# Moving the loads of the modulation weights and of the second branch's tiles from SyncE's queue to GpSimd's, in the merge of a hybrid diffusion layer

## The chip, the cores and the metric

The kernel runs on one core of one Trainium2 chip. The metric is the device time of one execution in microseconds (us); lower is better. The core has a matrix engine (TensorE, PE in the rows), VectorE (DVE), ScalarE (ACT), GpSimd (POOL) and SyncE (SP), each of which takes its own instructions in order, and 16 DMA engines that all queues share. A transfer is issued by an instruction in the queue of some engine; here nearly all of them stand in SyncE's.

## The reference, cut to what matters

One layer of a diffusion backbone: 1024 latent tokens and 256 context tokens of 1024 channels go through a mixer with two branches (a recurrent one, "A", and a state-space one, "B"), whose outputs are projected, gated and merged, and then through a gated MLP. All is float32. The parts around the change:

```python
mx = jnp.split((sc @ ada_w[l] + ada_b[l])[:, None, :], 6, axis=-1)       # six modulation vectors
...
g = (y * jax.nn.silu(z.astype(jnp.float32))).reshape(bsz, seqlen, SSD_GROUPS, SSD_INNER // SSD_GROUPS)
g = g * lax.rsqrt(jnp.mean(g * g, axis=-1, keepdims=True) + EPS)
return (g.reshape(bsz, seqlen, SSD_INNER) * norm_w.astype(jnp.float32)).astype(z.dtype)
...
def merge(ya, lg, yb, xs, z, gt):
    ra = ((ya[0] + ya[1]).astype(lg.dtype) * jax.nn.gelu(lg)) @ lru_proj
    rb = ssd_output(yb[0] + yb[1], xs, z, ssd_d, ssd_norm_w) @ ssd_proj
    ga, gb = jnp.split(jax.nn.sigmoid(gt), 2, axis=-1)
    return (ga * ra + gb * rb) @ w_out
...
x = x + mx[2] * ox
hx2 = modulate(rmsnorm(x, norm_ffn_w[l]), mx[3], mx[4])
x = x + mx[5] * conv_ffn(...)
```

The first two modulation vectors (`mx[0]`, `mx[1]`) are made at the start of the kernel; the other four (4096 values) are made inside the merge, and are first wanted by the residual add behind the output projection.

## The kernel before, in words

Channels lie on the 128 partitions and tokens along the free dimension. Precision is kept by splitting each float32 operand into a high part, which TensorE takes at full rate, and the remainder: a product is three matmuls, high by high, high by low, low by high (`gdense`, line 125). Splitting a tile is one copy on ScalarE (`act`, line 163) and one subtraction on VectorE (`tt`, line 160). So each weight tile of 128 output channels costs one load (`raw`, line 82), one ScalarE copy (`whi`), one VectorE subtraction (`wlo`), and 48 matmuls for 1024 tokens: 8 blocks of 128 input channels, 3 products, 2 halves of the tokens.

The merge (`merge`) has 24 such tiles, then the output projection `wout` follows:

- 8 tiles of `lru_proj`. Branch A's result, stored earlier to DRAM, is loaded tile by tile (`M<-ad`, line 1025) and split into the tiles `A` (even numbers high, odd numbers low); all eight are wanted by the first weight tile. Behind each tile the sigmoid of a gate (`sg`, `ga`, line 1034) multiplies the product into `M` on VectorE.
- 16 tiles of `ssd_proj`, in two halves of 8 of its 16 input blocks each. Ahead of each half, branch B's result is loaded from DRAM in pieces of 128x512 (`gk<-gd`, line 1050, 16 a half), multiplied by its norm's weight and the group's reciprocal root (`rsb<-rsd`, line 1045, one broadcast load for four pieces) in one VectorE instruction (line 157), and split: the first half into the tiles `H`, the second into `A` again. `gk` has two buffers, `rsb` one.

Beside this the remaining modulation is computed (`ada_rest`): `crow`, the conditioning vector on all partitions (line 338), through SiLU, then 32 times a load of a weight row block of 512 KB (`adar<-in_ada`, line 342) and one VectorE multiply-and-sum against `crow` (line 343), called a reduction below. `adar` has one buffer, so a load can't be issued before the reduction ahead of it is over. `ada_rest_end` adds the bias; `wout`'s first residual add waits for it.

Nobody writes the order by hand here. The program is recorded, and a scheduler sets the order of the instructions on each engine from its own estimate of when each can run; weight loads and splits have priority (`prio`). What each engine then runs is fixed: an instruction whose input is late holds all that stand behind it on its engine.

Of the kernel before, what the change touches and what calls it, by code (L numbers as in the profile page):

```python
# [15 lines left out]
P = 128  # L16
# [29 lines left out]
class Builder:  # L46
# [287 lines left out]
    def ada_rest(self, p1):  # L334

        nc, A = self.nc, self.A
        crow = self.t(p1, 1024, "crow")
        nc.sync.dma_start(crow, A["crows"][0].partition_broadcast(P))
        self.act(crow, crow, AF.Silu)
        for i in range(32):  # L340
            w = self.t(p1, 1024, "adar")
            nc.sync.dma_start(w, A["ada2"][i])
            nc.vector.tensor_tensor_reduce(w, w, crow, 1.0, 0.0, op0=ALU.mult, op1=ALU.add,
                                           accum_out=self.mods[:, 16 + i : 17 + i])
            yield
# [670 lines left out]
    def merge(self, pA, pM):  # L1016

        nc, tc, A = self.nc, self.tc, self.A
        F = self.FULL
        with tc.tile_pool(name="mg1", bufs=1) as p1, tc.tile_pool(name="mg2", bufs=2) as p2:  # L1020
            ah = [self.t(pA, T, f"A{2 * k}", F32R) for k in range(8)]
            al = [self.t(pA, T, f"A{2 * k + 1}", F32R) for k in range(8)]
            for k in range(8):
                ak = self.t(pM, T, f"M{k}")
                nc.sync.dma_start(ak, self.a_d[k])
                self.split(ak, ah[k], al[k])
            mm = [self.t(pM, T, f"M{k}") for k in range(8)]
            for m in range(8):
                w = self.wload(A["lrup"][m])
                ps = self.halves()  # L1030
                self.dense(ps, w, ah, al, F)
                for i, (s, e) in enumerate(F):
                    ga = self.gate_room(p1)
                    nc.sync.dma_start(ga, self.gate_d[m, :, s:e])
                    self.act(ga, ga, AF.Sigmoid)
                    self.tt(mm[m][:, s:e], ga, ps[i])
            rest = self.ada_rest(p1)
            for half in range(2):
                pool, nm = (self.pH, "H") if half == 0 else (pA, "A")
                yh = [self.t(pool, T, f"{nm}{2 * i}", F32R) for i in range(8)]  # L1040
                yl = [self.t(pool, T, f"{nm}{2 * i + 1}", F32R) for i in range(8)]
                for g in range(2):
                    for hf, (s, e) in enumerate(F):
                        rsb = self.t(p1, H, "rsb")
                        nc.sync.dma_start(rsb, self.rs_d[2 * half + g, 4 * hf : 4 * hf + 4].rearrange("c p -> (c p)")
                                          .partition_broadcast(P))
                        for i in range(4 * g, 4 * g + 4):
                            k = half * 8 + i
                            gk = self.t(p2, H, "gk")
                            nc.sync.dma_start(gk, self.g_d[k, :, s:e])  # L1050
                            self.stt(gk, gk, self.v("ssd_norm_w", k), rsb, op0=ALU.mult, op1=ALU.mult)
                            self.split(gk, yh[i][:, s:e], yl[i][:, s:e])
                for m in range(8):
                    w = self.wload(A["ssdp"][m, half])
                    ps = self.halves()
                    self.dense(ps, w, yh, yl, F)
                    for i, (s, e) in enumerate(F):
                        gb = self.gate_room(p1)
                        nc.sync.dma_start(gb, self.gate_d[8 + m, :, s:e])
                        self.act(gb, gb, AF.Sigmoid)  # L1060
                        self.tt(gb, gb, ps[i])
                        self.tt(mm[m][:, s:e], mm[m][:, s:e], gb, op=ALU.add)
                        next(rest, None)
            self.ada_rest_end()
            mh, ml = [], []
            for k in range(8):
                h = self.t(self.pH, T, f"H{2 * k}", F32R)
                l = self.t(self.pH, T, f"H{2 * k + 1}", F32R)
                self.act(h, mm[k], AF.Copy)
                self.tt(l, mm[k], h.bitcast(F32), op=ALU.subtract)  # L1070
                mh.append(h)
                ml.append(l)
        return mh, ml
# [502 lines left out]
```

## Time and profile before

| | |
|---|---|
| median of 3 runs | 2314.39 us (2313.72 to 2317.71) |
| the profiled execution's own time | 2316.08 us |
| its span in the profile | 2314.3 us |
| TensorE busy | 2238.8 us, 97% of the span |
| VectorE, ScalarE, GpSimd busy | 1640.5, 1150.1 and 330.0 us |
| moved by DMA | 274.88 MB, mean 119 GB/s |

A page of the profile gives busy time by engine, then the span in 40 slices, then the chain of work that ended last, then groups of equal instructions with their mean time and the idle time of their engine ahead of them. "SPq" is SyncE's queue of transfer issues. A row of a timeline gives its start in us from the start of the span, its length, engine, line and operation, and in brackets how long the engine had been idle and what ended that.

### The profile page before, as it was taken

How to read it: one execution, taken by the hardware profiler on the slowest of the kernel's cores; microseconds unless marked ns; L12 is line 12 of the kernel's file. 1: busy time of each engine (PE TensorE's matmuls, PEld its weight loads, DVE VectorE, ACT ScalarE, POOL GpSimd, SP SyncE). 2: the span in 40 equal slices, each digit the busy share in tenths (PEclk: the TensorE clock that was granted, in tenths of full speed). 3: DMA queues.
4: the chain of work that ended last, by engine and by line, in shares of the span. 5: the costliest groups of instructions: out<-in, count | busy, mean ns of one | idle time of the engine just before them, and what ended most of it. 6: DMA issues, size and time to landing. Idle time of an engine off the chain costs nothing.

```text
span 2314.3 us, 29745 instructions
## 1 busy us (share of the span) xinstructions
PE 2238.8 (97%) x11290; PEld 1852.4 (80%) x11290; DVE 1640.5 (71%) x2617; ACT 1150.1 (50%) x1781; POOL 330.0 (14%) x254
## 2 busy tenths in 40 slices
PE   6999999999999999999999999999889999999998
PEld 3778878778888888888888878888668888878888
DVE  4887877789978858767875675547877777774335
ACT  4577667667666647646635332334434444442121
POOL 0000000000000000000000000000757777740000
PEclk7999999999999999999999999999999999999999
DMA  6322322145335333524427775542022222244212
GB/s 250 96 69 73 95 83 65 62 126 159 122 107 172 114 121 106 159 85 130 155 90 267 234 231 191 171 139 73 28 73 82 83 82 82 80 161 129 77 55 73
DMA packets 87795, 274.88 MB, mean 119 GB/s; under 512 B 10434, under 2 KB 16610, under 8 KB 82404
## 3 DMA queue, kind: packets, MB, share of 16 engines
q1 hardware_dynamic: 87648, 272.97, 36.9%
q8 instruction: 89, 1.46, 0.3%
q14 instruction: 54, 0.44, 0.1%
q10 hardware_dynamic: 4, 0.01, 0.0%
HBM read 233.86 MB, written 39.08 MB: 118 GB/s over the span
## 4 chain that ended last, share of the span: by engine, by line
PE 76%; DVE 13%; DMA 5%; ACT 3%; issue 2%; POOL 1%; SPq 0%; POOLq 0%; DVEq 0%; ACTq 0%
PE d L125 30%; PE s L125 18%; PE d L1220 11%; PE s L1220 5%; PE s L986 2%; DMA adar<-in_ada 2%; PE s L651 2%; ACT L L163 1%; DVE wlo L160 1%; PE s L978 1%; DVE L L160 1%; DMA gk<-gd 1%; PE s L927 1%; PE s L926 1%; DVE facc L157 1%
## 5 line engine op out<-in xcount | busy, mean ns | idle before, releaser
L125 PE MATMUL d<-H,whi 128*128 128x512 f32 x2496 | 700.8, 398 | 1.8 <-DVE H L160 1.0
L125 PEld LDWEIGHTS d<-H,whi 128*128 128x128 f32 x2496 | 457.0, 188 | 97.1 <-issue 6.0
L125 PE MATMUL d<-H,wlo 128*128 128x512 f32 x1248 | 392.8, 393 | 1.8 <-DVE wlo L160 1.8
L163 ACT ACTIVATE whi<-raw 128x1024 fp32r<-128x1024 f32 (+2 forms) x194 | 185.7, 959 | 270.7 <-PE s L125 115.4
L125 PEld LDWEIGHTS d<-H,wlo 128*128 128x128 f32 x1248 | 232.9, 188 | 51.6 <-DVE wlo L160 3.5
L157 DVE SCALAR_TENSOR_TENSOR facc<-d,vec,facc 128x945 f32<-128x945 f32 (+2 forms) x176 | 214.6, 1221 | 72.9 <-ACT facc L163 68.6
L160 DVE TENSOR_TENSOR wlo<-raw,whi 128x1024 fp32r<-128x1024 f32 (+1 forms) x154 | 187.5, 1220 | 81.2 <-ACT whi L163 74.4
L125 PE MATMUL s<-H,whi 128*128 128x512 f32 x672 | 202.6, 390 | 1.9 <-ACT whi L163 1.9
L163 ACT ACT_TABLE_LOAD x102 | 130.9, 1283 | 85.9 <-DVE cacc L157 28.7
L1133 POOL TENSOR_TENSOR ssq<-H,A 128x512 f32<-128x512 f32 x4 | 6.0, 1493 | 1162.8 <-ACT H L163 1158.6
L125 PEld LDWEIGHTS s<-H,whi 128*128 128x128 f32 x672 | 125.8, 188 | 29.2 <-ACT whi L163 2.8
L125 PE MATMUL s<-A,whi 128*128 128x512 f32 x480 | 138.2, 390 | 1.0 <-POOL A L1133 1.0
L157 DVE SCALAR_TENSOR_TENSOR M<-s,mods,M 128x512 f32<-128x512 f32 (+1 forms) x72 | 49.5, 690 | 120.4 <-PE s L125 120.3
L125 PE MATMUL s<-H,wlo 128*128 128x512 f32 x336 | 126.0, 391 | 2.1 <-DVE wlo L160 2.0
L125 PEld LDWEIGHTS s<-A,whi 128*128 128x128 f32 x480 | 90.1, 188 | 20.1 <-POOL A L1133 1.4
L157 DVE SCALAR_TENSOR_TENSOR E<-E,cst 128x128 f32<-128x128 f32 x256 | 81.3, 344 | 20.5 <-ACT E L163 20.5
L163 ACT ACTIVATE m<-GU,dtt 128x128 f32<-128x128 f32 x256 | 78.7, 389 | 34.5 <-PE s L978 29.3
L157 DVE SCALAR_TENSOR_TENSOR m<-GL,dtt,m 128x128 f32<-128x128 f32 x256 | 77.7, 346 | 20.3 <-ACT m L163 20.1
L1220 PE MATMUL d<-A,whi 128*128 128x512 f32 x372 | 91.3, 395 | 0.0
L1220 PE MATMUL d<-A,wlo 128*128 128x512 f32 x348 | 85.9, 397 | 5.2 <-ACT ssq L163 5.2
L163 ACT ACTIVATE E<-E,cst 128x128 f32<-128x128 f32 x256 | 80.4, 389 | 17.5 <-DMA E<-csd 17.4
L125 PE MATMUL s<-A,wlo 128*128 128x512 f32 x240 | 83.1, 390 | 0.8 <-DVE wlo L160 0.8
(337 smaller groups left out, 4288.2 us busy)
## 6 DMA issues: line engine op xcount, KB each, us to landing
raw<-in_w SPq DMA_DIRECT2D x92, 512.0 KB, 3.6
E<-csd SPq DMA_DIRECT2D x32, 1024.0 KB, 7.1
A<-in_wup SPq DMA_DIRECT2D x40, 512.0 KB, 4.1
R<-csd SPq DMA_DIRECT2D x64, 256.0 KB, 4.7
adar<-in_ada SPq DMA_DIRECT2D x32, 512.0 KB, 4.0
hd<-facc SPq DMA_DIRECT2D x22, 512.0 KB, 5.1
gated<-sg SPq DMA_DIRECT2D x32, 256.0 KB, 3.8
gd<-y SPq DMA_DIRECT2D x32, 256.0 KB, 2.4
```

Of the source, the lines that this page charges most:

```text
L125: nc.tensor.matmul(o, a[:, k, :], b[k][:, xo + s : xo + e], start=(k == 0 and i == 0), stop=(k == kn - 1 and i == 2))
L157: self.pin(self.nc.vector.scalar_tensor_tensor(out, in0, s, in1, op0=op0, op1=op1))
L160: return self.pin(self.nc.vector.tensor_tensor(out, a, b, op=op))
L163: return self.pin(self.nc.scalar.activation(out, in_, f, **kw))
L651: nc.tensor.matmul(pg, a[:, q, :], b[:, s:e], start=(i == 0), stop=(i == 2))
L926: nc.tensor.matmul(ps[:, s - s2, 0, :], btok[:, s, :], xw[:, 0, s, :], start=True, stop=True)
L927: nc.tensor.matmul(ps[:, s - s2, 1, :], btok[:, 7 - s, :], xw[:, 1, 7 - s, :], start=True, stop=True)
L978: nc.tensor.matmul(psy[q, c, :], self.xt[:, c0 + c, q], m[:, h, c, :], start=True, stop=True)
L986: nc.tensor.matmul(pso[:, c, :], S[:, cc if d == 0 else 7 - cc, d, :], CT[:, cc * P : (cc + 1) * P], start=True, stop=True)
L1133: self.pin(self.nc.gpsimd.tensor_tensor(out, a, b, op=op))
L1220: q = self.pin(self.nc.tensor.matmul(ps, a[:, k, :], b, start=(k == 0 and i == 0 and p in ("11", "12", "s3")), stop=(k == 3 and i == 2), s ...
```

## The change

Four lines call another engine's queue: the loads of `crow`, `adar`, `rsb` and `gk` are issued by GpSimd instead of SyncE. 73 transfers move (1, 32, 8 and 32 of them). Tiles, buffers and arithmetic stay.

```diff
@@ ada_rest
         crow = self.t(p1, 1024, "crow")
-        nc.sync.dma_start(crow, A["crows"][0].partition_broadcast(P))
+        nc.gpsimd.dma_start(crow, A["crows"][0].partition_broadcast(P))
         self.act(crow, crow, AF.Silu)
         for i in range(32):
             w = self.t(p1, 1024, "adar")
-            nc.sync.dma_start(w, A["ada2"][i])
+            nc.gpsimd.dma_start(w, A["ada2"][i])
             nc.vector.tensor_tensor_reduce(w, w, crow, 1.0, 0.0, op0=ALU.mult, op1=ALU.add,
                                            accum_out=self.mods[:, 16 + i : 17 + i])
@@ merge
                         rsb = self.t(p1, H, "rsb")
-                        nc.sync.dma_start(rsb, self.rs_d[2 * half + g, 4 * hf : 4 * hf + 4].rearrange("c p -> (c p)")
+                        nc.gpsimd.dma_start(rsb, self.rs_d[2 * half + g, 4 * hf : 4 * hf + 4].rearrange("c p -> (c p)")
                                           .partition_broadcast(P))
                         for i in range(4 * g, 4 * g + 4):
                             k = half * 8 + i
                             gk = self.t(p2, H, "gk")
-                            nc.sync.dma_start(gk, self.g_d[k, :, s:e])
+                            nc.gpsimd.dma_start(gk, self.g_d[k, :, s:e])
```

Because the scheduler sees other queues, it also sets other orders. TensorE's is the same, row for row. Three places where the others differ follow.

**SyncE's and GpSimd's queues, where the moved loads begin.** Before, SyncE, from the first moved load on (`raw` is a weight tile, `gated` the stored gates):

```order
L1045 DMA rsb_10992<-rsd_3572 128x512
L82 DMA raw_10658<-in_lrup 128x1024
L1050 DMA gk_10994<-gd_3571 128x512
L1050 DMA gk_10999<-gd_3571 128x512
L829 DMA gated_93<-sg_10393 128x512
L338 DMA crow_11140<-in_crows 128x1024
L342 DMA adar_11143<-in_ada 128x1024
```

With the change, GpSimd, whose last instruction ahead of them fills a constant early in the state-space stage:

```order
L241 MEMSET btok_3726 64x4
L1045 DMA rsb_10992<-rsd_3572 128x512
L1050 DMA gk_10994<-gd_3571 128x512
L1050 DMA gk_10999<-gd_3571 128x512
L338 DMA crow_11140<-in_crows 128x1024
L342 DMA adar_11143<-in_ada 128x1024
L1050 DMA gk_11004<-gd_3571 128x512
L1050 DMA gk_11009<-gd_3571 128x512
L342 DMA adar_11151<-in_ada 128x1024
L1045 DMA rsb_11014<-rsd_3572 128x512
```

The moved loads now stand behind one another only; before, weight tiles and gates stood between them.

**VectorE, at the start of the merge** (`grsr` is the last norm of the state-space stage, `A` the splits of branch A that the first tile wants). Before:

```order
L160 TENSOR_TENSOR grsr_10243<-grsr_10243,grsa_10242 128x8
L160 TENSOR_TENSOR A_1384_10420<-M_1392_10428,A_1376_10412 128x1024
L160 TENSOR_TENSOR wlo_1410_10471<-raw_10468,whi_1409_10470 128x1024
L160 TENSOR_TENSOR A_1385_10421<-M_1393_10432,A_1377_10413 128x1024
L160 TENSOR_TENSOR A_1386_10422<-M_1394_10436,A_1378_10414 128x1024
L160 TENSOR_TENSOR A_1387_10423<-M_1395_10440,A_1379_10415 128x1024
L160 TENSOR_TENSOR A_1388_10424<-M_1396_10444,A_1380_10416 128x1024
L160 TENSOR_TENSOR A_1389_10425<-M_1397_10448,A_1381_10417 128x1024
L160 TENSOR_TENSOR wlo_1416_10534<-raw_10531,whi_1415_10533 128x1024
L160 TENSOR_TENSOR A_1390_10426<-M_1398_10452,A_1382_10418 128x1024
L160 TENSOR_TENSOR A_1391_10427<-M_1399_10456,A_1383_10419 128x1024
L157 SCALAR_TENSOR_TENSOR gk_10994<-gk_10994,vec_72,rsb_10992 128x512
```

With the change, from the row behind the same `grsr`:

```order
L157 SCALAR_TENSOR_TENSOR gk_10994<-gk_10994,vec_72,rsb_10992 128x512
L157 SCALAR_TENSOR_TENSOR gk_10999<-gk_10999,vec_72,rsb_10992 128x512
L160 TENSOR_TENSOR A_1384_10420<-M_1392_10428,A_1376_10412 128x1024
L160 TENSOR_TENSOR wlo_1410_10471<-raw_10468,whi_1409_10470 128x1024
L160 TENSOR_TENSOR A_1385_10421<-M_1393_10432,A_1377_10413 128x1024
L160 TENSOR_TENSOR A_1386_10422<-M_1394_10436,A_1378_10414 128x1024
L160 TENSOR_TENSOR A_1387_10423<-M_1395_10440,A_1379_10415 128x1024
L160 TENSOR_TENSOR H_1468_10984<-gk_10994,H_1460_10976 128x512
L160 TENSOR_TENSOR H_1469_10985<-gk_10999,H_1461_10977 128x512
L343 ISA adar_11143,mods_78<-adar_11143,crow_11140 128x1024
L343 ISA mods_78 128x1
L160 TENSOR_TENSOR A_1388_10424<-M_1396_10444,A_1380_10416 128x1024
```

Then come two more `gk` products, `A_1389`, `wlo_1416`, `A_1390`, `A_1391` and the second reduction. Work of branch B and a reduction now stand ahead of branch A's last four splits.

**VectorE, at the split of the fourth weight tile** (`wlo_1429`, from `raw_10658`). Before, two reductions stand ahead of it, of `adar_11143` and `adar_11151`:

```order
L160 TENSOR_TENSOR H_1471_10987<-gk_11009,H_1463_10979 128x512
L343 ISA adar_11151,mods_78<-adar_11151,crow_11140 128x1024
L343 ISA mods_78 128x1
L160 TENSOR_TENSOR M_1401_10461<-sg_10587,s_10537 128x512
L160 TENSOR_TENSOR M_1401_10461<-ga_10591,s_10538 128x512
L160 TENSOR_TENSOR wlo_1429_10661<-raw_10658,whi_1428_10660 128x1024
```

With the change five do, of `adar_11143`, `adar_11151`, `adar_11215`, `adar_11223` and `adar_11286`:

```order
L160 TENSOR_TENSOR H_1469_10985<-gk_11021,H_1461_10977 128x512
L343 ISA adar_11286,mods_78<-adar_11286,crow_11140 128x1024
L343 ISA mods_78 128x1
L157 SCALAR_TENSOR_TENSOR gk_11026<-gk_11026,vec_72,rsb_11014 128x512
L160 TENSOR_TENSOR M_1401_10461<-sg_10587,s_10537 128x512
L160 TENSOR_TENSOR wlo_1429_10661<-raw_10658,whi_1428_10660 128x1024
```

The count goes on by two for each tile in both. The last reduction, the 32nd, stands ahead of the split of the 19th tile before, and of the 18th with the change.

## Rows read from the trace of the kernel before

**Rows 1.** The page: busy us by engine (share of the span), instructions; granted clock in tenths.

```profile
PE 2238.8 (97%) x11290; PEld 1852.4 (80%) x11290; DVE 1640.5 (71%) x2617; ACT 1150.1 (50%) x1781; POOL 330.0 (14%) x254
...
PEclk7999999999999999999999999999999999999999
```

**Rows 2.** Windows over the merge, by stage: busy us (count) of each engine, clock, DMA share, GB/s.

```profile
1237.20:1325.50 88.30, 87.51 (x385) 71.92 (x384) 58.15 (x83) 35.58 (x49) 0.00 (x0) 1.00 0.74 242
1325.50:1422.10 96.60, 90.30 (x386) 71.43 (x385) 65.46 (x100) 26.22 (x38) 0.00 (x0) 1.00 0.68 222
1422.10:1509.00 86.90, 86.90 (x386) 71.93 (x385) 44.79 (x60) 26.93 (x34) 0.00 (x0) 1.00 0.55 175
```

**Rows 3.** Timeline of TensorE: first matmuls of merge and output projection, the longest stall.

```profile
1237.21 1.07 PE L125 MATMUL d<-A,whi 128*128 128x512 f32 x4
...
1338.28 1.20 PE L125 MATMUL s<-H,whi 128*128 128x512 f32 x4 [1.71 <-ACT whi L163]
...
1508.99 0.61 PE L125 MATMUL s<-H,whi 128*128 128x512 f32 x2
```

**Rows 4.** Chain that ended last, in the merge: start us, us, what (x48: one weight tile).

```profile
1340.98 5.33 DMA adar<-in_ada
1346.34 1.23 DVE adar L343
...
1433.00 10.88 PE s L125 x48
```

**Rows 5.** All waits from 1237 to 1480: engine, line, releaser, us, times, longest.

```profile
DVE adar L343 <- DMA adar<-in_ada: 40.8, 17, 4.7
```

**Rows 6.** Tile adar: instructions with ns min/median/max, first and last start; landing.

```profile
L342 SPq DMA_DIRECT2D adar<-in_ada x32: 327/333/478, 1244.7 to 1435.4; - x32
L343 DVE CUSTOM_DVE_ANT_0 adar<-adar,crow x32: 1211/1225/1228, 1253.5 to 1440.0; 128x1024 f32<-128x1024 f32 x32
...
DMA to landing us min/median/max: 3.4/4.0/4.5
```

**Rows 7.** Timeline of VectorE, start of the merge.

```profile
1226.23 1.23 DVE L160 TENSOR_TENSOR A<-M,A 128x1024 fp32r<-128x1024 f32 x1 [4.91 <-ACT A L163]
...
1229.25 3.49 DVE L160 TENSOR_TENSOR A<-M,A 128x1024 fp32r<-128x1024 f32 x3
...
1240.67 2.35 DVE L160 TENSOR_TENSOR A<-M,A 128x1024 fp32r<-128x1024 f32 x2
...
1253.45 1.22 DVE L343 CUSTOM_DVE_ANT_0 adar<-adar,crow 128x1024 f32<-128x1024 f32 x1
1254.60 0.08 DVE L343 DVE_READ_ACCUMULATOR2_ANT mods<- 128x1 f32 x1
```

**Rows 8.** Timeline of VectorE, the last reduction and the split of the 19th tile.

```profile
1440.03 1.23 DVE L343 CUSTOM_DVE_ANT_0 adar<-adar,crow 128x1024 f32<-128x1024 f32 x1 [4.63 <-DMA adar<-in_ada]
...
1442.21 1.22 DVE L160 TENSOR_TENSOR wlo<-raw,whi 128x1024 fp32r<-128x1024 f32 x1
```

**Rows 9.** Timeline of SyncE's queue, first loads of each kind in the merge.

```profile
1221.38 0.32 SPq L1025 DMA_DIRECT2D M<-ad  x1
...
1241.33 0.89 SPq L1050 DMA_DIRECT2D gk<-gd  x2
...
1254.71 0.33 SPq L342 DMA_DIRECT2D adar<-in_ada  x1
```

**Rows 10.** Tile gk: instructions with ns min/median/max, first and last start; landing.

```profile
L157 DVE SCALAR_TENSOR_TENSOR gk<-gk,vec,rsb x32: 741/747/755, 1246.5 to 1391.2; 128x512 f32<-128x512 f32 x32
...
L160 DVE TENSOR_TENSOR H<-gk,H x16: 681/686/696, 1248.0 to 1308.1; 128x512 fp32r<-128x512 f32 x16
...
DMA to landing us min/median/max: 3.1/4.6/7.9
```

**Rows 11.** GpSimd's instructions by line and shape: busy us, mean ns | idle before.

```profile
L1133 POOL TENSOR_TENSOR raw<-A 128x512 f32<-128x512 f32 x20 | 26.7, 1337 | 0.0
...
L238 POOL MEMSET btok<- 128x512 f32 x1 | 0.5, 531 | 16.9 <-DVE ge L160 16.9
```

## The prediction, made before the changed kernel ran

> **What bounds the kernel now.** First the page: TensorE is busy for 2238.8 us of 2314.3, at the full clock of 2.4 GHz in all but the first of 40 slices [rows 1]. So anything that the change can give must come from the few places where TensorE waits, and anything that it costs must make TensorE wait. I then cut the merge into windows, since all moved loads lie there [rows 2]. In its first part TensorE is busy for 87.5 of 88.3 us, in the last for all of it, in the middle one for 90.3 of 96.6. GpSimd does nothing in any of them. The timeline gives the merge's ends: its first matmul starts at 1237.21, the first of the output projection at 1508.99 [rows 3], which makes 271.8 us. One weight tile takes 10.88 us where nothing is late [rows 4], and 24 of them 261.1. **10.7 us, 0.46%, is thus the most that a faster merge can give**; the longest single stall of it is 1.71 us [rows 3].
>
> Next, what TensorE waits for. Its stalls end with the split of a weight tile, on ScalarE or VectorE, and the chain of waits leads from there through VectorE to loads of `adar` and the reductions that consume them [rows 4]. VectorE stood still for 40.8 us, 17 times, until an `adar` load had landed [rows 5]. As `adar` has one buffer, this is a loop: the reduction (1.22 us, and a readout of 0.08) ends at 1254.68, the next load is issued at 1254.71 [rows 7, 9], and lands 4.0 us after its issue in the median [rows 6]. Bare, a turn is 0.03 + 4.0 + 1.30 = 5.3 us. The first reduction starts at 1253.45 and the 32nd at 1440.03 [rows 7, 8]: 186.58 us over 31 turns, **6.02 us a turn**, so 0.7 us a turn is other VectorE work that stands in the way. Two turns a tile are 12.0 us against TensorE's 10.88. That loses 1.2 us a tile, first out of the lead that the splits have, then, in the middle window, out of TensorE's time. At the end no lead is left: the split behind the last reduction is over at 1443.43 [rows 8], and the tile that wants it starts when the one before it ends, at 1443.88 [rows 4].
>
> **The change, part by part.**
>
> *Issues taken from SyncE.* 73 at 0.33 us each [rows 6] are 24 us off a queue. I cost this at nothing, because the loop shows that an `adar` load went out 0.03 us after its buffer was free: SyncE was not late for it. Were it late elsewhere, the gain would end at the 10.7 us above.
>
> *The start.* GpSimd has nothing else to do, so its first loads need only wait until their memory is free of the stage before, as SyncE's first load of the merge did until 1221.38; `gk` went out at 1241.33 [rows 9]. That is 20 us sooner, but what it is worth is set by VectorE's new order. There two `gk` products stand ahead of branch A's first split. Issued from 1221.4 behind `rsb`, with the median landing of 4.6 us [rows 10], the pair is there at about 1227 to 1228.5, and the products take 2 x 0.75; the first split, at 1226.23 before [rows 7], so starts near 1229.5. Four splits were over at 1232.74 before [rows 7], now near 1236. Then two `H` splits (2 x 0.69) free both buffers at 1237.5, and the first reduction is over by about 1240. The second `gk` pair can be issued only then: landing at about 1243, products to 1244.5, and behind them four VectorE instructions of 1.2 us to the end of `A_1391`, near 1249.5 (before: 1240.67 + 2.35 = 1243.0 [rows 7]). One to two us more for branch A's loads, which now share the DMA engines with 1.8 MB of moved loads (one `rsb`, two `gk`, `crow`, `adar`) while those are already busy for 0.7 of the time [rows 2]. **The second reduction starts near 1251.** TensorE wants `A_1391` at 1237.21 + 7 x 1.36 + 0.45 = 1247.2 (eight blocks a tile, two matmul steps into the last), so it waits here for 2 to 4 us; this delay is part of the sum below and not added to it.
>
> *The order.* Of the 32 reductions the last stands ahead of the 18th tile's split instead of the 19th's. The same reduction is therefore due one tile, 10.9 us, sooner.
>
> *The loop.* From the second reduction to the 32nd are 30 turns, at 6.02 + x, where x is what a load costs more from GpSimd between a free buffer and the landing. 1251 + 30 x 6.02 = 1431.6, which is 8.4 us ahead of 1440.0; less the 10.9 that it is due sooner, TensorE is **2.5 us later, plus 30x**, and as no lead was left at the end before, all of it is lost.
>
> *x.* No row shows GpSimd issuing a transfer. The lower end is 0: as quick as SyncE. For the upper end I take its elementwise work on 128x512, 1.34 us [rows 11], as if building a transfer of 128 rows cost as much. Nearest in kind is an instruction in which GpSimd only writes to 128 partitions and reads nothing, its memset of 128x512, **0.53 us** [rows 11], counted whole, since it comes ahead of the transfer. 2.5 + 30 x 0.53 = **18.4 us**. The Trainium skill, "DMA: Bandwidth & Descriptors", section "Latency and other measured facts", speaks against the change in the same direction: it puts the first byte at about 600 ns from SyncE's kind of queue and about 1 us from GpSimd's, whose software writes the descriptors; by that, as an estimate, x were 0.4 and the sum 14.5 us. No run here shows it yet.
>
> *The half tiles of branch B.* 16 `gk` a half go through the same queue. Their last `H` split starts at 1308.1 [rows 10], and the tiles that want it start eight tiles, 87 us, behind the merge's first matmul, near 1324; 16 us of lead cover 16 loads that are each up to 0.53 us later, 8.5 us in all. At x over 1 this cover is gone. The bias add and `sc2`, behind the last reduction, come 60 us ahead of the output projection's first use: nothing.
>
> **The sum.** 2316.1 (the profiled execution's own time) + 18.4 = 2334.5. The median of the runs shown is 1.7 us lower than that execution, so I predict **2332.8 us**. A change of 0.2%, 4.6 us, is about what a measurement of this kernel can tell from none.
>
> **Rivals.**
>
> *The issue is hidden (x near 0).* GpSimd is idle and could issue as fast as SyncE; the transfers then land as before, and only the start and the order are left: 2.5 us, 2316.9, no change. For it: the same 16 DMA engines carry the bytes, and SyncE's issue is only 0.33 us long. Against it: a turn can hide nothing, since it is a loop with one buffer. The Trainium skill, same page, section "Issuing engines are not separate DMA queues", says that where transfers are issued changes only the sequencer's time, usually small; by that, this would be the likeliest. The trace bears it out for SyncE alone.
>
> *Faster: a turn gets shorter.* Moved loads no longer stand behind weight tiles and gates in SyncE's queue. If that were what makes a turn 6.02 instead of the bare 5.3, then 2.5 - 30 x 0.7 = -18.5, of which TensorE can take 10.7: 2303.7. It decides from x below -0.08, where 2.5 + 30x passes zero. Against it: the issue 0.03 us behind the free buffer, and that VectorE, not SyncE, holds the 0.7.
>
> *GpSimd is far slower (x of 1 or more).* Each load runs on it one behind the other, two `gk` ahead of an `adar`, and in that queue a load whose buffer isn't free holds the next, whose buffer may be. At x = 1 it is 32.5 us, 2346.9; at 1.34, 42.7 us, 2357.1, and branch B's half tiles are late as well. For it: GpSimd's elementwise work on 128x512 takes 1.34 us where VectorE's takes 0.69 [rows 10, 11].
>
> **How the numbers follow.** The forecast (x from 0.15 to 1) has 0.67: the loop is seen in the rows, its longer turn is not. Hidden 0.14, faster 0.06, far slower 0.13. Range: below the forecast it takes in the hidden case, from 2317, and leaves out the faster one; above, it goes to x = 1.2 (2352.9) and leaves out the rest of the slow case, 0.06 or so. Faster by over 0.2%: 0.05. Within: hidden and the mildest of the faster case, 0.15. Slower: 0.80.
>
> **What would show it.** In the changed profile 27.8 MB should go through a second DMA queue. The first reduction should start near 1240, the second near 1251, the last near 1448, a turn being about 6.5 us; VectorE's wait for `adar` should grow from 40.8 us by some 15. The output projection's first matmul should come near 1527, with TensorE's stalls in all parts of the merge and none behind it. A turn of 6.0 us or less, or stalls that don't end with VectorE's or ScalarE's split of a weight tile, would make the reasoning wrong; a turn much over 7 only the size of x.

## The result, and the profile after

The changed kernel takes 2335.87 us (median of 5 runs, 2333.36 to 2337.44), the kernel before beside it 2317.71 (2313.72 to 2320.95): a ratio of 1.0082, 95% interval 1.0071 to 1.0094. It is **18.2 us slower** by the medians (19.0 by the ratio); the sum of the prediction was 18.4. Its profiled execution took 2335.64 us with a span of 2333.9.

The page of the changed kernel, busy time, granted clock and DMA queues (packets, MB, share of 16 engines):

```profile
PE 2245.6 (96%) x11290; PEld 1855.1 (79%) x11290; DVE 1639.7 (70%) x2617; ACT 1148.4 (49%) x1780; POOL 368.9 (16%) x327
...
PEclk8999999999999999999999999999999999999999
...
q1 hardware_dynamic: 77136, 245.18, 32.7%
q0 software_dynamic: 7952, 27.79, 3.8%
```

The change did what it says: 27.79 MB go through a second queue, and GpSimd has 73 instructions more than in [rows 1]. The same windows over the merge as in [rows 2]:

```profile
1237.20:1325.50 88.30, 80.38 (x341) 64.79 (x340) 56.28 (x79) 33.78 (x46) 17.14 (x32) 0.96 0.74 241
1325.50:1422.10 96.60, 87.13 (x366) 68.81 (x365) 62.22 (x94) 24.79 (x37) 16.68 (x32) 0.98 0.65 206
1422.10:1509.00 86.90, 85.17 (x372) 69.15 (x372) 44.08 (x61) 25.57 (x32) 2.53 (x5) 1.00 0.50 162
```

TensorE is busy for 252.7 us of these 271.8, before for 264.7: 12.0 us more idle. And its granted clock, 1.00 throughout before, is 0.96 and 0.98 in the first two windows: 0.04 x 88.3 + 0.02 x 96.6 = 5.5 us of full clock lost. Both together, 17.5 us, are what the merge grew by, as the timeline of TensorE shows (first matmul of the merge, its longest stall, its last one, first matmul of the output projection):

```profile
1239.74 1.16 PE L125 MATMUL d<-A,whi 128*128 128x512 f32 x4 [0.22 <-issue]
...
1251.43 1.22 PE L125 MATMUL d<-A,whi 128*128 128x512 f32 x2 [4.19 <-DVE A L160]
...
1453.48 0.73 PE L125 MATMUL s<-A,wlo 128*128 128x512 f32 x2 [1.07 <-DVE wlo L160]
...
1528.88 0.61 PE L125 MATMUL s<-H,whi 128*128 128x512 f32 x2
```

1528.88 - 1239.74 = 289.1 us, against 271.8 in [rows 3]: 17.4 us longer. I call this the merge's length and use it for every run below, since the start of the merge itself lies at 1234 to 1241 from one execution to another, with the same work ahead of it (in `order_alone` alone the first matmul waits, experiment 2). The last stall ends with the split behind the last reduction.

VectorE's timeline in the changed kernel, start of the merge and last reduction:

```profile
1231.14 0.75 DVE L157 SCALAR_TENSOR_TENSOR gk<-gk,vec,rsb 128x512 f32<-128x512 f32 x1 [7.67 <-DMA gk<-gd]
...
1242.56 1.23 DVE L343 CUSTOM_DVE_ANT_0 adar<-adar,crow 128x1024 f32<-128x1024 f32 x1 [0.94 <-ACT crow L163]
...
1248.40 0.75 DVE L157 SCALAR_TENSOR_TENSOR gk<-gk,vec,rsb 128x512 f32<-128x512 f32 x1 [3.46 <-DMA gk<-gd]
...
1254.70 1.22 DVE L343 CUSTOM_DVE_ANT_0 adar<-adar,crow 128x1024 f32<-128x1024 f32 x1
1255.84 0.08 DVE L343 DVE_READ_ACCUMULATOR2_ANT mods<- 128x1 f32 x1
...
1449.44 1.23 DVE L343 CUSTOM_DVE_ANT_0 adar<-adar,crow 128x1024 f32<-128x1024 f32 x1 [4.09 <-DMA adar<-in_ada]
```

The first reduction comes 2.8 us behind the merge's first matmul, the second 15.0, the last 209.7 (before: 202.8, [rows 3, 8]). From the second to the last are 30 turns of (1449.44 - 1254.70) / 30 = **6.49 us**, before 6.02. GpSimd's timeline says where a part of that comes from:

```profile
1256.22 0.53 POOL L342 DMA_DIRECT2D adar<-in_ada  x1 [5.15 <-DVE mods L343]
...
1261.79 0.53 POOL L342 DMA_DIRECT2D adar<-in_ada  x1 [3.83 <-DVE mods L343]
```

The readout ends at 1255.92 and GpSimd starts its issue 0.30 us later, where SyncE took 0.03 [rows 7, 9]; it is so in all 31 turns here, and in 30 of 31 before. The issue holds GpSimd for 0.53 us, SyncE for 0.33. VectorE's waits from 1215 to 1540, and the landing of `adar` behind its issue:

```profile
DVE adar L343 <- DMA adar<-in_ada: 47.2, 21, 5.3
DVE gk L157 <- DMA gk<-gd: 23.4, 12, 7.7
...
DVE gk L157 <- DMA rsb<-rsd: 6.8, 4, 2.8
```

```profile
L342 POOL DMA_DIRECT2D adar<-in_ada x32: 527/533/540, 1226.6 to 1445.0; - x32
...
DMA to landing us min/median/max: 3.6/4.3/10.9
```

The same waits in the kernel before, of which only that for `adar` is in [rows 5] (the second from the tile `gk`):

```profile
DVE gk L157 <- DMA gk<-gd: 16.2, 10, 3.5
...
  DMA rsb<-rsd: 2.7, 1
```

So the wait for `adar` grew by 6.4 us only, those for `gk` and `rsb` by 7.2 and 4.1. The total came out as forecast, its parts did not, and that is what the experiments are about.

### The profile page after: what moved, and what is told of

Same layout as the page of the kernel before. It is cut to its first block, busy times and chain, and to the rows that moved or that the text cites. A ratio compares the mean times of both kernels' runs of the same rounds, so it can differ in the third digit from the quotient of the medians.

```text
span 2333.9 us, 29765 instructions
## 1 busy us (share of the span) xinstructions
PE 2245.6 (96%) x11290; PEld 1855.1 (79%) x11290; DVE 1639.7 (70%) x2617; ACT 1148.4 (49%) x1780; POOL 368.9 (16%) x327
## 3 DMA queue, kind: packets, MB, share of 16 engines
q0 software_dynamic: 7952, 27.79, 3.8%
## 4 chain that ended last, share of the span: by engine, by line
PE 71%; DVE 12%; issue 9%; ACT 3%; DMA 2%; POOL 2%; POOLq 0%; SPq 0%; DVEq 0%; ACTq 0%
PE d L125 27%; PE s L125 17%; PE d L1220 11%; PE s L1220 4%; PE s L986 2%; ACT L L163 2%; PE s L651 2%; DVE L L160 1%; PE s L978 1%; DVE wlo L160 1%; PE s L927 1%; DVE facc L157 1%; PE s L926 1%; PE s L309 1%; DVE L L157 1%
## 5 line engine op out<-in xcount | busy, mean ns | idle before, releaser
L157 DVE SCALAR_TENSOR_TENSOR M<-s,mods,M 128x512 f32<-128x512 f32 (+1 forms) x72 | 49.5, 690 | 119.9 <-PE s L125 119.8
L1220 PE MATMUL d<-A,whi 128*128 128x512 f32 x372 | 91.2, 395 | 0.0
L125 PE MATMUL d<-A,whi 128*128 128x512 f32 x288 | 81.6, 401 | 6.0 <-DVE A L160 4.2
```

The source lines that it names most:

```text
L125: nc.tensor.matmul(o, a[:, k, :], b[k][:, xo + s : xo + e], start=(k == 0 and i == 0), stop=(k == kn - 1 and i == 2))
L157: self.pin(self.nc.vector.scalar_tensor_tensor(out, in0, s, in1, op0=op0, op1=op1))
L1220: q = self.pin(self.nc.tensor.matmul(ps, a[:, k, :], b, start=(k == 0 and i == 0 and p in ("11", "12", "s3")), stop=(k == 3 and i == 2), s ...
```

## The experiments

Each ran in 5 rounds beside the kernel before. In three groups of four kernels its medians were 2314.99, 2317.00 and 2315.40 us; a difference in us below is the ratio's distance from 1 times that, by which the changed kernel is 19.0 us slower.

**1. The queue without the new order.** The scheduler moved instructions on TensorE, VectorE and ScalarE because the loads moved. `queue_alone` takes the changed kernel and ties these engines to the order of the kernel before (176 instructions of VectorE and 82 of ScalarE, by edges that set the order of issue and add no wait; TensorE's order then comes out the same):

```diff
+def in_order(nc, tc):
+    made = {i.name: i for i in nc.cur_bb.bb.instructions}
+    for row in ORDER:
+        for a, b in zip(row, row[1:]):
+            tc.add_manual_dep(made[f"I-{b}"], f"I-{a}", mybir.DependencyInfo(
+                mybir.DependencyClass.NoSync, mybir.DependencyReason.DATA), reason="order")
```

> The 73 loads are issued by GpSimd, while VectorE, ScalarE and TensorE run their instructions in exactly the order of the kernel before. Theory (the loop: an adar turn is about 0.47 us longer on GpSimd's queue, 6.49 against 6.02): 31 turns at 0.47 make it about 14.6 us slower than the kernel before (11 to 17), a turn stays near 6.5 us, and TensorE has no 4 us stall at the merge's start. Rival 1 (the new order on VectorE costs it, the queue is hidden): within 3 us of the kernel before, a turn of 6.0 us. Rival 2 (branch B's pieces come late): slower, but with stalls only at the tiles that want H or A from gk.

Ratio 1.0054 (1.0040 to 1.0067): **12.5 us slower**. Tile `adar` and the waits of VectorE:

```profile
L343 DVE CUSTOM_DVE_ANT_0 adar<-adar,crow x32: 1218/1226/1227, 1257.0 to 1455.1; 128x1024 f32<-128x1024 f32 x32
...
DMA to landing us min/median/max: 3.7/4.1/11.7
```

```profile
DVE adar L343 <- DMA adar<-in_ada: 47.5, 20, 5.0
...
DVE gk L157 <- DMA gk<-gd: 13.2, 8, 3.0
...
DVE gk L157 <- DMA rsb<-rsd: 7.6, 2, 4.5
```

A turn is (1455.1 - 1257.0) / 31 = 6.39 us, 0.37 longer than before with the same instructions in the same order; the merge takes 283.3 us, 11.5 more. That the order costs all of it is refuted. Taken this way, the queue is two thirds of the loss and the new order the rest, 17.4 - 11.5 = 5.9 us.

**2. The order without the queue.** `order_alone` is the kernel before, all loads on SyncE, tied to the changed kernel's order on VectorE, on ScalarE (the same 82 instructions) and on TensorE's first two tiles.

> All loads stay on SyncE's queue, while VectorE, ScalarE (to the middle of the merge) and TensorE run in the order of the changed kernel. Theory (the loop): a turn stays at 6.0 us, so only the start and the order remain, 2 to 6 us slower than the kernel before, with the stall of about 4 us at A_1391 and few later ones. Rival 1 (the order): 15 us or more slower, near the changed kernel. What could spoil the reading: in this order SyncE issues gk and adar loads ahead of weight loads and holds those while it waits for a buffer; then a turn or a weight load is late by SyncE's own waiting, seen in its issue long after the buffer came free.

Ratio 1.0067 (1.0054 to 1.0080): 15.5 us slower, a miss of my theory. The first row of VectorE in the merge, TensorE's first matmul and a later stall there, and the reductions:

```profile
1240.26 0.75 DVE L157 SCALAR_TENSOR_TENSOR gk<-gk,vec,rsb 128x512 f32<-128x512 f32 x1 [18.53 <-DMA gk<-gd]
```

```profile
1243.26 2.04 PE L125 MATMUL d<-A,whi 128*128 128x512 f32 x4 [5.48 <-issue]
...
1256.29 0.83 PE L125 MATMUL d<-A,whi 128*128 128x512 f32 x2 [3.07 <-DVE A L160]
```

```profile
L343 DVE CUSTOM_DVE_ANT_0 adar<-adar,crow x32: 1216/1225/1227, 1249.1 to 1446.4; 128x1024 f32<-128x1024 f32 x32
```

VectorE stands for 18.5 us at a piece of branch B, ahead of branch A's first split, because SyncE issues that piece's load behind branch A's own. The order was made for a queue that issues it at once, and it isn't cheap without one. So this run doesn't price the order as part of the changed kernel; experiment 1 does, by the difference. The two don't add up, 12.5 and 15.5 us against 19.0 for both, so that split is one way of taking them apart. And a turn is (1446.4 - 1249.1) / 31 = 6.36 us here, on SyncE's queue, where a load goes out 0.03 us behind the readout in 29 of 31 turns: a longer turn is not by itself the mark of GpSimd's queue.

**3. A longer turn on purpose.** `double_issue` puts a memset of half the buffer ahead of each `adar` load on GpSimd, in the changed kernel's order:

```diff
-            nc.gpsimd.dma_start(w, A["ada2"][i])
+            nc.gpsimd.memset(w[:, :H], 0.0), nc.gpsimd.dma_start(w, A["ada2"][i])
```

> The changed kernel with one more GpSimd instruction ahead of each adar load, a memset of half its buffer (0.53 us), in the changed kernel's order on VectorE and ScalarE. Theory (the loop, no lead left): each of 30 turns is longer by 0.55 to 0.7 us, near 7.1 us, so the kernel is 16 to 21 us slower than the changed one, 34 to 39 us slower than the kernel before. Rival 1 (GpSimd's issue is hidden, the order costs it): at most 3 us slower than the changed kernel. Rival 2 (branch B's pieces come late): some of it, but then gk waits grow more than adar waits.

Ratio 1.0138 (1.0124 to 1.0152): 31.9 us slower than before, some 13 more than the changed kernel. Its tile `adar`:

```profile
L342 POOL MEMSET adar<- x32: 524/526/530, 1226.6 to 1458.7; 128x512 f32 x32
...
L343 DVE CUSTOM_DVE_ANT_0 adar<-adar,crow x32: 1219/1225/1226, 1243.3 to 1464.0; 128x1024 f32<-128x1024 f32 x32
```

The second reduction starts at 1255.78, so a turn is (1464.0 - 1255.8) / 30 = 6.94 us: 0.45 more, and 30 x 0.45 = 13.5 us. With the memset the issue starts 0.88 us behind the readout instead of 0.30, so about three quarters of a delay of 0.59 us go into the end; my 16 to 21 took it for entirely whole. That the issue is hidden is refuted here as well.

**4. and 5. Half of the loads each.** `pieces_only` moves only `gk` and `rsb`, `weights_only` only `crow` and `adar` (the other lines stay `nc.sync`, and the scheduler orders each anew).

> Only branch B's loads (gk and rsb, 40 of them) go through GpSimd; the adar loop stays with SyncE. Theory (the loop): a turn stays near 6.0 us; the scheduler puts gk products ahead of the A splits as in the changed kernel, so a stall of some us at the merge's start may remain, but it is not lost at the end, since the 32nd reduction is due ahead of the 19th tile's split as before: 0 to 5 us slower. Rival 2 (branch B's pieces come late): 13 us or more slower. Rival 1 (the order at the start): 4 us or more slower, with the start's stall kept to the end.

> Only the modulation weights (crow and adar, 33 loads) go through GpSimd; branch B's pieces stay with SyncE. Theory as revised by the first four runs (a turn of the adar loop is longer by the issue on GpSimd, about 0.25 us, and by VectorE's waits for pieces and rsb that stand inside the loop, and the loads that GpSimd issues at once delay branch A's): the reductions begin some 20 us sooner, a turn is 6.2 to 6.4 us, the 32nd reduction is in time for the tile that wants it; what is left is a start later by 1 to 4 us: 1 to 8 us slower than the kernel before, about half of the changed kernel's loss or less. Rival 1 (the issue on GpSimd alone makes the loss, 0.47 us a turn): 13 us or more slower.

Ratios 1.0085 (1.0072 to 1.0099) and 1.0114 (1.0095 to 1.0132): 19.7 and 26.4 us slower. **Either half alone costs as much as both or more.** My theory had expected 0 to 5 and 1 to 8. In `pieces_only` the `adar` loop is SyncE's as before, and still a turn takes (1454.3 - 1255.9) / 31 = 6.40 us. Its tile `adar` and VectorE's waits:

```profile
L343 DVE CUSTOM_DVE_ANT_0 adar<-adar,crow x32: 1217/1224/1228, 1255.9 to 1454.3; 128x1024 f32<-128x1024 f32 x32
```

```profile
DVE adar L343 <- DMA adar<-in_ada: 36.9, 15, 5.2
DVE gk L157 <- DMA gk<-gd: 33.9, 16, 8.6
DVE gk L157 <- DMA rsb<-rsd: 14.9, 5, 4.8
```

and in `weights_only`, its waits and those of SyncE's queue:

```profile
DVE gk L157 <- DMA gk<-gd: 43.2, 16, 4.2
DVE adar L343 <- DMA adar<-in_ada: 42.6, 13, 11.3
```

```profile
SPq L1050 <- DVE H L160: 44.5, 16, 6.3
```

In both it is less the wait for `adar` that grew (36.9 and 42.6 us, before 40.8) than that for `gk` (33.9 and 43.2, before 16.2): its two buffers are a loop like that of `adar` (split, issue, landing, product, split), and in these orders the products stand between the reductions, so that VectorE waits for them as well. A turn is thus not the `adar` loop plus x, as I had it; it is the sum of VectorE's work and of whatever load it stands at next. In `weights_only` that is 7.08 us, from 1241.68 to 1454.14 in 30 turns. Which loads VectorE meets late hangs, as I read it, on the order that the scheduler derives from the queues; no run holds the order of these two kernels fixed, so this is argued and not shown.

**6. A second buffer for `rsb`**, the changed kernel's order kept on TensorE, VectorE and ScalarE:

```diff
-    BUFS = {"L": 10, "adaw": 3, "raw": 2, "cacc": 4, "csg": 2, "row": 3, "xdg": 4}
+    BUFS = {"L": 10, "adaw": 3, "raw": 2, "cacc": 4, "csg": 2, "row": 3, "xdg": 4, "rsb": 2}
```

> The changed kernel with two buffers for rsb instead of one, so that the broadcast load of the next group doesn't wait for the last product of this one; the order on TensorE, VectorE and ScalarE is that of the changed kernel. Theory as revised (VectorE's in-order waits for late pieces and rsb lengthen the adar loop): the wait for rsb falls from 6.8 us to under 1, part of it comes back as wait for adar, and the kernel is 2 to 6 us faster than the changed one, 12 to 16 us slower than the kernel before. Rival 1 (only the issue of adar counts): within 1.5 us of the changed kernel, all of the rsb wait coming back as adar wait.

Ratio 1.0057 (1.0040 to 1.0074): 13.2 us slower than before, some 6 faster than the changed kernel (the two intervals touch). VectorE waits for `rsb` only once, 5.1 us ahead of its first product; `adar` has 49.5 us of wait, 2.3 more than in the changed kernel. The merge takes 284.5 us, 4.6 less. So waits for pieces inside the loop are lost time too: the part of the loss that this takes away was never in the issue of `adar`.

**7. The bare queue.** `queue_bare` is `queue_alone` with two `rsb` buffers, and with the first loads on GpSimd held until branch A's last tile has been copied:

```diff
+    for a in ["I-10993", "I-10995", "I-11000", "I-11141", "I-11144", "I-11015"]:
+        tc.add_manual_dep(made[a], "I-10458", mybir.DependencyInfo(
+            mybir.DependencyClass.Sync, mybir.DependencyReason.DATA), reason="start")
```

> As queue_alone (all moved loads on GpSimd, every engine in the order of the kernel before), and with the two other effects taken away: rsb has two buffers, and the first rsb, gk, crow and adar loads wait until branch A's last tile has landed and been copied, as late as SyncE issued them. What remains is the longer bare turn of the adar loop. Theory: 31 turns at 0.2 to 0.3 us, 5 to 9 us slower than the kernel before, the first reduction 32 us behind the last instruction of the stage before, as in the kernel before, and VectorE's wait for rsb near 0. Rival 1 (the issue is the whole of it, rsb and the start are nothing): 11 us or more slower, as queue_alone. Rival 3 (the issue is hidden, rsb and the start were all of it): within 3 us of the kernel before.

Ratio 1.0051 (1.0037 to 1.0065): 11.8 us slower, as much as `queue_alone` and more than the 5 to 9 that I had expected, so what I took away was worth nothing in that order. Tile `adar`, and a wait of VectorE:

```profile
L343 DVE CUSTOM_DVE_ANT_0 adar<-adar,crow x32: 1216/1226/1228, 1253.0 to 1449.8; 128x1024 f32<-128x1024 f32 x32
```

```profile
DVE gk L157 <- DMA gk<-gd: 23.0, 10, 5.5
```

31 turns of (1449.8 - 1253.0) / 31 = 6.35 us: with VectorE's wait for `rsb` gone and none of GpSimd's loads beside branch A's first, a turn is still **0.33 us** longer than SyncE's. Most of that can be seen directly. From the free buffer to the issue GpSimd takes 0.295 us in every turn, SyncE 0.028 in 30 of 31: **0.27 us** more, 8.3 us in 31 turns. Behind the issue no difference is sure. A load lands 4.1 us after its issue began in the median, before 4.0 [rows 6], but the trace of the kernel before tells the landing of only 7 of its 32 loads; from the issue to a reduction that waited for it, the median is 4.45 us here, 4.18 in `queue_alone` and 4.38 before. What is left of a turn, 0.06 to 0.1 us, can as well be VectorE's wait for `gk`, 23.0 us here and 16.2 before, since those loads moved too; no run moves the `adar` loads alone in the old order. So x is 0.27 us as far as it is shown, and with experiment 1 at most 0.33 to 0.37. The Trainium skill, "DMA: Bandwidth & Descriptors", section "Latency and other measured facts", has the first byte at about 0.6 us from one kind of queue and about 1 us from the other, by estimate 0.4 us apart; no run here shows a first byte, and the 0.27 us that the runs do show lie ahead of the issue.

**8. Two loads in flight.** `half_loads` cuts each `adar` load and reduction of the changed kernel in two, with two buffers of half the size; the second halves' sums go to a column of their own and are added at the end.

```diff
-            w = self.t(p1, 1024, "adar")
-            nc.gpsimd.dma_start(w, A["ada2"][i])
...
+            for h in range(2):
+                w = self.t(p1, H, "adar")
+                nc.gpsimd.dma_start(w, A["ada2"][i][:, h * H : h * H + H])
...
```

> The changed kernel with each adar load and reduction cut into two of 512 columns, and two buffers of that size in the same memory; one more VectorE add at the end joins the sums. 64 loads, of which one is in flight while the other is reduced. Theory (the single buffer makes the turn): VectorE's wait for adar falls from 47 us to under 25, and the kernel is 4 to 12 us faster than the changed one, although VectorE has some 10 us more work and the scheduler puts the last reduction two tiles sooner. Rival 2 (the pieces are what holds VectorE): within 3 us of the changed kernel or slower.

Ratio 1.0120 (1.0101 to 1.0139): 27.8 us slower, a miss. The tile `adar`:

```profile
L344 DVE CUSTOM_DVE_ANT_0 adar<-adar,crow x64: 682/689/694, 1237.0 to 1423.2; 128x512 f32<-128x512 f32 x64
```

```profile
1419.64 0.69 DVE L344 CUSTOM_DVE_ANT_0 adar<-adar,crow 128x512 f32<-128x512 f32 x1 [2.64 <-DMA adar<-in_ada]
```

A row block now takes (1423.2 - 1237.0) / 31 = 6.0 us, so the loop did become faster. But the scheduler, which sees two buffers, puts the first half of the last row block, the row at 1419.64, ahead of the 15th tile's split, where the changed kernel has its last reduction ahead of the 18th's. That half starts 185.4 us behind the merge's first matmul (1234.2), 24.3 us sooner than the last reduction of the changed kernel, and is due three tiles, 32.6 us, sooner: 8.3 us late, and the merge is 297.5 us long, 8.4 more than that of the changed kernel. A faster loop is worth nothing where the order asks for more than it gives.

**9. to 12. Reductions spread out.** If TensorE is late because reductions stand in front of splits faster than their loads can come, they should stand farther apart. The 32 reductions are taken up from the first of the 24 tiles on, three in two tiles, at distances of one, a half and a half tile (the expectations call it four in three), and kept behind what the program has ahead of them:

```diff
-            nc.vector.tensor_tensor_reduce(w, w, crow, 1.0, 0.0, op0=ALU.mult, op1=ALU.add,
-                                           accum_out=self.mods[:, 16 + i : 17 + i])
-            yield
+            q = nc.vector.tensor_tensor_reduce(w, w, crow, 1.0, 0.0, op0=ALU.mult, op1=ALU.add,
+                                               accum_out=self.mods[:, 16 + i : 17 + i])
+            yield self.tc.keep_in_program_order(q)
...
-                        next(rest, None)
+                        if i == 0 or m % 2:
+                            next(rest, None)
```

and the same call behind each half of the first eight tiles. `paced_gpsimd` does it to the changed kernel, `paced_sync` to the kernel before; `paced_three_gk` is `paced_sync` with `"gk": 3` in `BUFS`; `paced_weights_gpsimd` is `paced_sync` with `crow` and `adar` on GpSimd.

> All moved loads on GpSimd as in the changed kernel, but the 32 reductions are spread over the 24 tiles of the merge, four in three tiles, and VectorE can't run one ahead of the product that stands ahead of it in the program. Theory (TensorE is late because reductions, each bound to a turn of 6 us or more, stand in front of weight splits faster than TensorE uses tiles): a reduction is wanted every 8.2 us on average, over any turn seen so far, so TensorE has no stalls in the middle of the merge; left is a stall of 2 to 5 us at the start, where a piece of branch B still stands ahead of branch A's first split: 4 us faster to 2 us slower than the kernel before. Rival (transfers collide, or weight tiles themselves are late on GpSimd's account): 10 us or more slower, as the changed kernel.

> All loads on SyncE as before, and the 32 reductions spread over the 24 tiles of the merge in the same way. Theory: no stall of TensorE in the middle of the merge, and none at its start, since branch A's splits stand ahead of branch B's pieces: the merge nears its floor of 261.1 us, 6 to 11 us faster than the kernel before. Rival (the middle's stalls come from SyncE's queue or from VectorE's total work, not from the reductions' place): within 3 us of the kernel before.

> paced_sync with three buffers for gk instead of two. Theory (what is left of TensorE's stalls in paced_sync comes from VectorE standing at a piece of branch B that hasn't landed, 25.8 us in all): that wait falls under 15 us, and the kernel is 1 to 4 us faster than paced_sync, 5 to 10 us faster than the kernel before. Rival (the wait only moves to other loads): within 1 us of paced_sync.

> paced_sync with crow and adar on GpSimd's queue, branch B's pieces on SyncE's. Theory (the longer turn costs only where the loop is dense; paced_gpsimd lost by pieces that stood behind an adar load in GpSimd's queue): within 3 us of paced_sync, 2 to 9 us faster than the kernel before, with a stall of up to 2 us at the start, since crow and adar are loaded beside branch A. Rival 1 (the issue on GpSimd costs of itself): 7 us or more slower than paced_sync.

| | ratio, 95% interval | us | merge's length |
|---|---|---|---|
| `paced_gpsimd` | 1.0049 (1.0031 to 1.0067) | +11.4 | 278.4 |
| `paced_sync` | 0.9982 (0.9971 to 0.9992) | -4.2 | 269.7 |
| `paced_three_gk` | **0.9954 (0.9942 to 0.9967)** | -10.7 | 261.2 |
| `paced_weights_gpsimd` | 1.0042 (1.0029 to 1.0054) | +9.7 | 275.6 |

`paced_three_gk` is faster than both kernels. Its windows, and VectorE's waits:

```profile
1237.20:1325.50 88.30, 88.30 (x392) 73.10 (x391) 58.18 (x83) 34.17 (x50) 0.00 (x0) 1.00 0.76 249
1325.50:1422.10 96.60, 96.60 (x428) 79.95 (x427) 64.20 (x95) 26.61 (x39) 0.00 (x0) 1.00 0.61 197
```

```profile
DVE adar L343 <- DMA adar<-in_ada: 29.1, 16, 4.4
DVE gk L157 <- DMA gk<-gd: 26.2, 9, 8.1
```

In the merge TensorE doesn't stand still once, and it takes the 24 x 10.88 = 261.1 us that the prediction had as its floor. The gain of 10.7 us is a little more than the 5 to 10 expected, and the reason was another: the wait for `gk` didn't fall under 15 us, it is as long as in `paced_sync` (25.8). VectorE still waits for its loads, only where no split that TensorE needs stands behind. In `paced_sync` TensorE's idle time in the three windows falls from 7.1 us to 4.8 only, less than I expected. The third buffer without the pacing was not run, so what it gives alone stays open. With GpSimd's queue the pacing doesn't reach the kernel before, a miss of both expectations, and both runs lose again behind the merge, where TensorE waits 4.32 and 3.13 us for a split of the merged tiles. A distance of half a tile, 5.4 us, is nearer to a bare turn on SyncE than on GpSimd; but how much of these 9.7 and 11.4 us is that, and how much the late splits behind the merge, no run tells. It stays open.

## Why the prediction was right, step by step

*Issues taken from SyncE:* nothing is seen to come back from them; no run tests this by itself. SyncE was at hand 0.03 us behind the readout in 30 of 31 turns, as the prediction says of one; once it came 2.3 us late.

*The start:* first and second reduction were forecast 2.8 and 13.8 us behind the merge's first matmul, and came 2.8 and 15.0 behind it. TensorE's stall at a split of branch A was to be 2 to 4 us; it was 4.19.

*The order:* the account that the kernel is late by what the last reduction is late, plus the tile by which it is due sooner, holds: 209.7 - 202.8 + 10.9 = 17.8 us against the 17.4 by which the merge grew. The order's own part was under-sized: 2.5 us forecast, 5.9 by experiment 1.

*The loop:* a turn of 6.55 us was forecast, 6.49 measured, in 30 turns. In `queue_alone` the same account gives (1455.1 - 1239.8) - 202.8 = 12.5, measured 11.5.

*x:* this is the term that was mis-sized. 0.53 us, all of it the GpSimd issue, was to show as 15 us more wait for `adar`. The wait grew by 6.4, and x is 0.27 us as far as it is shown, 8.3 us in 31 turns, at most 0.37. The row that I took as nearest, a memset of 0.53 us [rows 11], happens to equal the time for which an issue holds GpSimd, but a load isn't late by that: counted from the start of the issue it lands as soon as one of SyncE's, as far as the trace tells, and what is late is that start. The rest of a turn's 0.47 us, 0.1 to 0.2, I put down to waits for `gk` and `rsb`, which grew by 11.3 us together. The loop's 15.9 us of the sum were 11.5 by experiment 1, the order's 2.5 were 5.9, and the two errors nearly cancelled. That a loop in which nothing overlaps gets longer and that all of it is lost at the end was right; that 18.4 met 18.2 was luck.

*The half tiles of branch B:* that they are covered by a lead of 16 us was right for TensorE and wrong for VectorE, which stands at them in order, with a reduction and a weight's split behind. Experiment 6 shows some 6 us of it.

The rival *the issue is hidden* falls by experiments 1, 3 and 7. *Faster* falls with the turn. *Far slower* had neither the size nor the mechanism: in the changed kernel every `adar` load went out 0.30 us and every `gk` load at most 0.54 us after its buffer was free, so no load was held long behind another. The Trainium skill, "DMA: Bandwidth & Descriptors", section "Issuing engines are not separate DMA queues", says that issuing from several engines saves only the time in which an engine issues, usually small beside the transfer. Here the runs differ from that: 73 loads on another queue made the kernel 0.8% slower, and 0.5% with the old order on TensorE, VectorE and ScalarE. No run issued the loads from a third engine, so what is priced is GpSimd's issue and not a second queue as such.

## What to carry to other kernels

Before a load is moved to another queue, see who stands waiting for it: a load into a single buffer is a loop, and 0.27 us more between a free buffer and the issue come back at every turn. Where a scheduler sets the order, moving a load also moves the work on the engines that consume it, and a load that an in-order engine meets too early holds the critical work behind it; cost the new order by itself. The cure here was neither queue nor issue but distance: side work spread along the tiles and one buffer more for the pieces together took the merge's last stall of TensorE; spread along the tiles alone it gave 4.2 us of the 10.7.

## What the runs showed of the hardware that I had not expected

The granted clock of TensorE falls behind some of its stalls. Three windows of the changed kernel behind the stall of 4.19 us:

```profile
1248.00:1252.00 4.00, 0.57 (x1) 0.50 (x2) 3.26 (x4) 3.81 (x6) 0.54 (x1) 0.67 0.66 254
1252.00:1256.00 4.00, 4.00 (x11) 3.11 (x10) 4.00 (x6) 1.07 (x3) 0.00 (x0) 0.50 0.79 198
1256.00:1260.00 4.00, 4.00 (x19) 3.31 (x18) 1.13 (x2) 1.06 (x1) 1.60 (x3) 0.98 0.77 239
```

In the second TensorE is busy throughout at 0.50, the lower level of 1.2 GHz. `pieces_only` shows the same behind a stall of 2.23 us that ended at 1300.83, and over its merge:

```profile
1304.00:1308.00 4.00, 4.00 (x11) 3.02 (x11) 1.84 (x3) 1.20 (x2) 1.07 (x2) 0.50 0.88 250
```

```profile
1237.20:1325.50 88.30, 81.48 (x331) 65.33 (x330) 52.53 (x74) 32.62 (x43) 10.72 (x20) 0.92 0.72 237
1325.50:1422.10 96.60, 87.31 (x360) 68.78 (x359) 62.64 (x95) 25.02 (x37) 9.11 (x17) 0.96 0.64 208
```

That is 0.08 x 88.3 + 0.04 x 96.6 = 10.9 us of full clock, more than half of the 19.4 us by which its merge is longer (291.2 us), while TensorE's idle time grew by 9.6 only. In the kernel before, with no stall over 1.71 us, the clock stays at 1.00. Length alone doesn't decide: a stall of 2.78 us in the changed kernel, ended at 1352.78, left the clock as it was.

Whether the lower clock made the kernel longer is another question, and nothing here shows that it did. From 1244 to 1453 us VectorE waits for TensorE not once, in the changed kernel and in `pieces_only`, and ScalarE once in each, for 4.1 and 0.7 us, near the merge's start. In the changed kernel TensorE's last stall in the merge still ends with a split on VectorE (1453.48, 1.07 us), and from there to the merge's end the clock is full. A faster TensorE ahead of that split would, as I read it, have waited longer there and gone on at the same time. So the lost clock tells where the 17.5 us of the merge went and is hardly a second cause of them: my sum, which goes by VectorE's last reduction, had no term for it and came out without one.
